# Order of the high products in feature-major steps, and four compression taps side by side

## The chip, the cores and the metric

The kernel runs on one core of a Trainium2 chip. The metric is the time of one execution on the device in microseconds. A core has TensorE (PE in the profile, its weight loads PEld), VectorE (DVE), ScalarE (ACT), GpSimd (POOL) and SyncE (SP, which here issues nearly all DMAs). Each runs its own instructions in order and waits for the others by semaphores.

## The reference

The reference is a decoder trunk of four layers on 256 tokens of 1024 features, float32. Each layer is `x = x + mixer(rms_norm(x))`, then `x = x + square(relu(rms_norm(x) @ w_up)) @ w_down` with 4096 hidden features. The mixers are native sparse attention (NSA), stick-breaking attention, a convolution module, and block-sparse attention.

What the change touches in the first mixer is the compression of keys and values. For 2 groups of heads, each of 15 windows of 32 tokens (a window starts every 16 tokens) is reduced to one vector:

```
n_cmp = (S - L) // STR + 1                      # 15, with L = 32 and STR = 16
cidx = cmp_start[:, None] + jnp.arange(L)[None, :]
kc = einsum('bnlgd,lde->bnge', kc[:, cidx] + cmp_pos[0][None, None, :, None, :], w_cmp[0])
vc = einsum('bnlgd,lde->bnge', vc[:, cidx] + cmp_pos[1][None, None, :, None, :], w_cmp[1])
...
p_c = _masked_softmax(einsum('bqghd,bngd->bqghn', qc, kc) * scale, ...)
o_c = einsum('bqghn,bngd->bqghd', p_c, vc)
```

So a window is a sum over 32 positions ("taps") of a token's vector plus a position vector, times that tap's own 128 x 128 matrix.

## The kernel before, in words

Activations are feature-major (features on partitions) in `xr`. Every projection is made of float32r products: weights arrive by DMA as float32 (`raw`, 1 MB, three buffers), ACT rounds them to a high part `wh` (L155) and DVE subtracts to a low part `wl` (L156); activations are split the same way, and three products are summed: high by high, high by low, low by high.

`proj_T` makes feature-major results. It is used for the up projections of all four MLPs and for queries and keys of the stick-breaking layer. `wh` is the stationary operand against both parts of the activations at once (512 columns, L200), `wl` against the high part (256 columns, L201). Two features of 128 rows are made together, each in its own PSUM bank: in each of the eight steps `kt` first the one feature's two products are issued, then the other's. `proj` makes token-major results with three products of 512 columns (`mm3`, L180 to L182), as the down projection does.

NSA runs as six column chunks of its projection: keys and values for the compression (chunk 0, transposed to `kcT` by `transpose_to`), the other keys (1), four heads of queries (2), values and gates (3), the remaining heads (4, 5). `compress` stands between chunk 3 and the first `attend`. For keys and then values, DVE adds the position vectors to all windows (`win`, L532, two instructions), and 32 float32 matmuls of 30 columns by 128 (L540) sum the taps in PSUM (`pc`); a float32 matmul is two records in the trace. The taps' matrices come in four transfers of 1 MB (`rawc`, L537) into the same three `raw` buffers. For the keys the result is copied (`kk`), transposed and copied into columns 256 to 286 of `kcat`, which `scores` reads; between products and copy, `flush` issues twelve pending transposes (L450). For the values it is copied to `vcmp`, which `mix` reads.

`attend` goes through units (head, half of the tokens): `scores` (mask and score products, maxima on DVE, exponentials on ACT, weights on DVE) and one unit later `mix` (transposes and value products). A scheduler at build time sets the final order on each engine; so products of chunks 4 and 5 stand between the units' instructions.

Of the kernel before, what the change touches and what calls it, by code (L numbers as in the profile page):

```python
# [10 lines left out]
F32 = mybir.dt.float32  # L11
# [55 lines left out]
def trunk(ctx: ExitStack, tc: tile.TileContext, A: dict, out: bass.AP):  # L67
# [8 lines left out]
    def bank(tag, name):  # L76
        return ps.tile([P, 512], F32, tag=tag, bufs=4 if tag == "B" else 2, name=name)
# [116 lines left out]
    def proj_T(aT, v, fs):  # L194

        os_ = [bank("B", "projT") for f in fs]
        for kt in range(KT):
            for o, f in zip(os_, fs):
                c = slice(f * P, (f + 1) * P)
                nc.tensor.matmul(o, lhsT=v[kt][0][:, c], rhs=aT[:, kt], start=kt == 0, stop=False)  # L200
                nc.tensor.matmul(o[:, :S], lhsT=v[kt][1][:, c], rhs=aT[:, kt, 0], start=False, stop=kt == KT - 1)  # L201
        return os_
# [211 lines left out]
    def nsa(n, first):  # L414
        aT = n.xT
        nxt = start_norm(4)
        with tc.tile_pool(name="nsa", bufs=1) as sp:
# [13 lines left out]
            nc.vector.memset(kcat[:, :, 256:288], 0.0)  # L431
            nc.vector.memset(vcmp, 0.0)
            oT = act.tile([P, KT, 2, NT, P], F32R, tag="aT", name="oT")
            with tc.tile_pool(name="nsw", bufs=2) as wp:
# [11 lines left out]
                def transpose_to(dsts, srcs):  # L446
                    def go():
                        pt = bank("B", "pt")
                        for i, s_ in enumerate(srcs):
                            nc.tensor.transpose(pt[:, i * P:(i + 1) * P], s_, ident)  # L450
                        for d_, (a, b) in dsts:
                            nc.scalar.copy(d_, pt[:, a * P:b * P].rearrange("p (a b) -> p a b", b=P))

                    waiting.append(go)
# [9 lines left out]
                kcT = wp.tile([P, 2, 2, S], F32, tag="kcT", bufs=1, name="kcT")  # L464
# [5 lines left out]
                def chunk(ci):  # L470
# [10 lines left out]
                    for t in range(NT):  # L481
# [4 lines left out]
                        if ci == 0:  # L486
# [5 lines left out]
                            transpose_to([(kcT[:, 0, :, ts_], (0, 2)), (kcT[:, 1, :, ts_], (2, 4))],  # L492
# [24 lines left out]
                def tables():  # L517
                    nc.sync.dma_start(mks, A["nsa_mask"])
                    nc.vector.tensor_copy(mk, mks)
                    nc.gpsimd.tensor_copy(identr, ident)  # L520
                    nc.sync.dma_start(posT, A["nsa_pos"])

                def compress():

                    for kv in range(2):
                        win = wp.tile([P, 960], F32, tag="win", bufs=1, name="win").rearrange(
                            "p (l g n) -> p l g n", g=2, n=15)
                        kc = kcT[:, kv]
                        for g in range(2):
                            src = bass.AP(tensor=kc.tensor, offset=kc.offset + g * S,  # L530
                                          ap=[kc.ap[0], [1, 32], [16, 15]])
                            nc.vector.tensor_tensor(win[:, :, g], src,  # L532
                                                    posT[:, kv, :, None].to_broadcast([P, 32, 15]), op=ALU.add)
                        pc = bank("B", "pc")
                        for hf in range(2):
                            raw = rawp.tile([P, 2048], F32, tag="raw", name="rawc")
                            nc.sync.dma_start(raw, A["nsa_cmp"][:, kv, hf * 2048:(hf + 1) * 2048])  # L537
                            for l in range(16):
                                ll = hf * 16 + l
                                nc.tensor.matmul(pc[:30, :DH], lhsT=win[:, ll].rearrange("p a b -> p (a b)"),  # L540
                                                 rhs=raw[:, l * DH:(l + 1) * DH], start=ll == 0, stop=ll == 31)
                        if kv == 0:
                            flush()
                            kk = wp.tile([32, DH], F32, tag="kk", bufs=1, name="kk")
                            nc.scalar.copy(kk[:30], pc[:30, :DH])
                            pt = bank("B", "pt")
                            nc.tensor.transpose(pt[:, :30], kk[:30], ident[:30, :30])
                            for g in range(2):
                                nc.scalar.copy(kcat[:, g, 256:286], pt[:, :30])
                        else:  # L550
                            nc.scalar.copy(vcmp[:30], pc[:30, :DH])
# [95 lines left out]
                compress()  # L647
                attend([(h, t) for t in range(NT) for h in range(4)])
# [421 lines left out]
def _constants():  # L1070
# [14 lines left out]
    for t in range(NT):  # L1085
        for g in range(2):
            m = np.full((P, 32), NEG)
            for n in range(15):
                m[:, 15 * g + n] = np.where(16 * n + 31 <= t * P + i, 0.0, NEG)
            mask.append(m)  # L1090
# [3 lines left out]
    tri = np.stack([np.where(i[:, None] >= i[None, :], -1.0, 0.0), np.full((P, P), -1.0)], 1).astype(np.float32)  # L1094
    return {
        "ident": np.eye(P, dtype=np.float32), "rope": rope, "causal": causal,
# [4 lines left out]
def _layout(x):  # L1101
# [23 lines left out]
    a["nsa_cmp"] = np.ascontiguousarray(f["nsa_w_cmp"][0].transpose(2, 0, 1, 3).reshape(P, 2, -1))  # L1125
# [37 lines left out]
```

## Time and profile before

| | |
|---|---|
| median of 3 runs (lowest, highest) | 1221.04 us (1220.31, 1221.4) |
| the profiled execution: its own time, its span | 1220.13 us, 1218.2 us |
| PE busy | 1196.0 us (98%), 7009 records |
| weight loads busy | 1023.7 us (84%) |
| DVE busy | 781.0 us (64%) |
| ACT busy | 628.4 us (52%) |
| POOL busy | 28.3 us (2%) |
| read from HBM | 207.73 MB, 172 GB/s over the span |
| mean granted clock of TensorE | 0.997 |

Matmuls overlap: a record's duration is longer than the distance to the next start. What a matmul costs in a dense stream is read from start to start. The timeline merges neighbours of one line and shape; "x64" are then 64 records from the first start to the last end.

### The profile page before, as it was taken

To read this page: it belongs to the slowest core of one execution; us is meant where nothing else is said; L and a number is where in the kernel's file an instruction comes from. 1 tells how busy PE (TensorE), PEld (TensorE's weight loads), DVE (VectorE), ACT (ScalarE), POOL (GpSimd) and SP (SyncE) were. 2 spreads that over 40 slices of the span, in tenths; PEclk is the share of its full clock that TensorE was granted. 3 is DMA by queue.
4 is the path that set the end of the run, shared out by engine and by line. 5 is a ranking of instruction groups with operands and counts; after the bars stand their busy time and mean duration, and the time that the engine had idled before them with its cause. 6 is when DMAs were issued, how large, how long until landed. Compare 5 with 4: busy or idle time off the path is not lost.

```text
span 1218.2 us, 17586 instructions
## 1 busy us (share of the span) xinstructions
PE 1196.0 (98%) x7009; PEld 1023.7 (84%) x7009; DVE 781.0 (64%) x1208; ACT 628.4 (52%) x1035; POOL 28.3 (2%) x36
## 2 busy tenths in 40 slices
PE   7999999999999999999999989999999999999998
PEld 5888888888888898888888869888888879888887
DVE  7877685565585479555665258655657886755563
ACT  6376664444465555444563256444446655545341
POOL 0100000000000000000000000000001010000000
PEclk9999999999999999999999989999999999999999
DMA  7544064554554425554546326545544643545540
GB/s 288 183 174 163 16 231 169 207 203 147 203 181 153 162 90 202 199 206 171 189 160 255 123 78 246 185 173 207 199 144 174 238 139 105 207 155 196 202 173 35
DMA packets 33777, 211.09 MB, mean 173 GB/s; under 512 B 4256, under 2 KB 6304, under 8 KB 10144
## 3 DMA queue, kind: packets, MB, share of 16 engines
q1 hardware_dynamic: 31104, 203.99, 46.9%
q0 software_dynamic: 1152, 4.70, 1.1%
q10 hardware_dynamic: 1440, 1.28, 0.3%
q8 instruction: 55, 0.90, 0.3%
q14 instruction: 26, 0.21, 0.0%
HBM read 207.73 MB, written 2.23 MB: 172 GB/s over the span
## 4 chain that ended last, share of the span: by engine, by line
PE 92%; DVE 4%; ACT 1%; POOL 1%; DMA 1%; issue 1%; SPq 0%; ACTq 0%; DVEq 0%; POOLq 0%
PE projT L200 22%; PE projT L201 11%; PE dn L180 10%; PE dn L182 10%; PE dn L181 10%; PE ab L859 4%; PE proj L180 3%; PE proj L181 3%; PE proj L182 3%; PE acc L207 3%; PE acc L208 2%; PE acc L209 2%; PE cv L793 2%; DVE wl L156 2%; PE pc L540 1%; PE po L626 1%
## 5 line engine op out<-in xcount | busy, mean ns | idle before, releaser
L156 DVE TENSOR_TENSOR wl<-raw,wh 128x1024 fp32r<-128x1024 f32 (+2 forms) x376 | 445.7, 1210 | 205.3 <-ACT wh L155 204.7
L155 ACT CAST wh<-raw 128x1024 fp32r<-128x1024 f32 (+2 forms) x376 | 379.7, 1041 | 213.3 <-PE dn L182 112.5
L200 PE MATMUL projT<-xT,wh 128*128 128x512 f32 x1152 | 407.9, 398 | 0.3 <-DVE xT L100 0.3
L201 PE MATMUL projT<-xT,wl 128*128 128x256 f32 x1152 | 323.0, 281 | 0.0
L200 PEld LDWEIGHTS projT<-xT,wh 128*128 128x128 f32 x1152 | 216.3, 188 | 53.0 <-DVE xT L100 0.5
L201 PEld LDWEIGHTS projT<-xT,wl 128*128 128x128 f32 x1152 | 217.4, 189 | 1.1
L180 PE MATMUL dn<-wh,u 128*128 128x512 f32 x512 | 201.4, 393 | 0.0
L182 PE MATMUL dn<-wh,u 128*128 128x512 f32 x512 | 200.3, 391 | 0.0
L181 PE MATMUL dn<-wl,u 128*128 128x512 f32 x512 | 200.1, 391 | 0.0
L182 PEld LDWEIGHTS dn<-wh,u 128*128 128x128 f32 x512 | 96.2, 188 | 21.2
L180 PEld LDWEIGHTS dn<-wh,u 128*128 128x128 f32 x512 | 96.2, 188 | 20.5
L181 PEld LDWEIGHTS dn<-wl,u 128*128 128x128 f32 x512 | 96.3, 188 | 19.6
L300 ACT COPY b<-projT 128x256 f32<-128x256 f32 x128 | 46.9, 373 | 93.2 <-PE projT L201 89.5
L180 PE MATMUL proj<-wh,xT 128*128 128x512 f32 (+2 forms) x224 | 87.0, 389 | 7.7 <-ACT wh L155 7.7
L181 PE MATMUL proj<-wl,xT 128*128 128x512 f32 (+2 forms) x224 | 86.0, 384 | 0.0
L182 PE MATMUL proj<-wh,xT 128*128 128x512 f32 (+2 forms) x224 | 85.3, 382 | 0.0
L301 DVE TENSOR_TENSOR s<-projT,b 128x256 f32<-128x256 f32 x128 | 51.4, 421 | 50.3 <-ACT b L300 50.1
L88 ACT CAST u<-q 128x1024 fp32r<-128x1024 f32 x32 | 33.6, 1050 | 82.1 <-DVE q L303 82.1
L207 PE MATMUL acc<-oT,wh 128*128 128x256 f32 x256 | 74.0, 294 | 1.9 <-ACT oT L88 1.9
L208 PE MATMUL acc<-oT,wh 128*128 128x256 f32 x256 | 74.1, 291 | 0.4 <-DVE oT L89 0.4
L209 PE MATMUL acc<-oT,wl 128*128 128x256 f32 x256 | 71.6, 288 | 0.0
L89 DVE TENSOR_TENSOR u<-q,u 128x1024 fp32r<-128x1024 f32 x32 | 39.2, 1225 | 33.5 <-ACT u L88 33.5
(257 smaller groups left out, 1273.7 us busy)
## 6 DMA issues: line engine op xcount, KB each, us to landing
raw<-in_up SPq DMA_DIRECT2D x64, 1024.0 KB, 4.8
raw<-in_down SPq DMA_DIRECT2D x64, 1024.0 KB, 4.9
raw<-in_sb_w SPq DMA_DIRECT2D x12, 1024.0 KB, 4.8
raw<-in_moba_w SPq DMA_DIRECT2D x12, 1024.0 KB, 4.9
raw<-in_conv_w SPq DMA_DIRECT2D x8, 1024.0 KB, 4.9
st<-dr POOLq DMA_DIRECT2D x8, 574.0 KB, 4.2
raw<-in_nsa_w SPq DMA_DIRECT2D x4, 1024.0 KB, 5.9
rawc<-in_nsa_cmp SPq DMA_DIRECT2D x4, 1024.0 KB, 5.0
```

What stands on the lines that cost most here:

```text
L155: nc.scalar.copy(wh[:, :w], r)
L156: nc.vector.tensor_sub(wl[:, :w], r, wh[:, :w].bitcast(F32))
L180: nc.tensor.matmul(o, lhsT=aT[:, kt, 0, t, :], rhs=wh, start=first, stop=False)
L181: nc.tensor.matmul(o, lhsT=aT[:, kt, 0, t, :], rhs=wl, start=False, stop=False)
L182: nc.tensor.matmul(o, lhsT=aT[:, kt, 1, t, :], rhs=wh, start=False, stop=last)
L200: nc.tensor.matmul(o, lhsT=v[kt][0][:, c], rhs=aT[:, kt], start=kt == 0, stop=False)
L201: nc.tensor.matmul(o[:, :S], lhsT=v[kt][1][:, c], rhs=aT[:, kt, 0], start=False, stop=kt == KT - 1)
L207: nc.tensor.matmul(o, lhsT=wh, rhs=aT[:, kt, 0], start=first, stop=False, skip_group_check=True)
L208: nc.tensor.matmul(o, lhsT=wh, rhs=aT[:, kt, 1], start=False, stop=False, skip_group_check=True)
L209: nc.tensor.matmul(o, lhsT=wl, rhs=aT[:, kt, 0], start=False, stop=last, skip_group_check=True)
L301: nc.vector.tensor_add(s[:, f], o[:, :S], b)
L859: nc.tensor.matmul(os_[f][:, i * S:(i + 1) * S], lhsT=v[kt][wi][:, fs], rhs=aT[:, kt, xi], start=kt == 0 and m == 0 and i == 0, stop=kt == ...
```

## The change

In `proj_T` the loop over the two features moves inside the loop over the two parts: high, high, low, low instead of high, low, high, low.

In NSA `kcT` changes its layout: for each of 16 residues r of the token number there are 36 columns; columns 1 to 32 hold the 16 tokens `16 n + r` of both groups, column 0 and column 33 the two position vectors of taps r and 16 + r, the rest is zero. A slice of 32 neighbouring columns is then a stationary operand as it stands, and no windows are built. Four taps go to four groups of 32 output rows of one PSUM bank; their sum, with the shift by one window and the position vectors' products, is made by one more matmul with a constant 0/1 matrix `quarters`, which for the keys also transposes. Position vectors and zeros are written by POOL, `quarters` comes by its own DMA of 16 KB. The masks and the order of the tap matrices in memory are permuted to match. `compress(1)`, the values' part, is called before the second unit of `attend`.

```
 def proj_T(aT, v, fs):
         for kt in range(KT):
-            for o, f in zip(os_, fs):
-                c = slice(f * P, (f + 1) * P)
-                nc.tensor.matmul(o, lhsT=v[kt][0][:, c], rhs=aT[:, kt], start=kt == 0, stop=False)
-                nc.tensor.matmul(o[:, :S], lhsT=v[kt][1][:, c], rhs=aT[:, kt, 0], start=False, stop=kt == KT - 1)
+            for part, width in enumerate((2 * S, S)):
+                rhs = aT[:, kt] if part == 0 else aT[:, kt, 0]
+                for o, f in zip(os_, fs):
+                    nc.tensor.matmul(o[:, :width], lhsT=v[kt][part][:, f * P:(f + 1) * P], rhs=rhs,
+                                     start=kt == 0 and part == 0, stop=kt == KT - 1 and part == 1)
...
-                kcT = wp.tile([P, 2, 2, S], F32, tag="kcT", bufs=1, name="kcT")
+                kcT = wp.tile([P, 2, 16, 36], F32, tag="kcT", bufs=1, name="kcT")
...
-                            transpose_to([(kcT[:, 0, :, ts_], (0, 2)), (kcT[:, 1, :, ts_], (2, 4))],
+                            cols = [kcT[:, kv, :, 1 + 16 * t:17 + 16 * t].rearrange("p r (n g) -> p g n r", g=2)
+                                    for kv in range(2)]
+                            transpose_to([(cols[0], (0, 2)), (cols[1], (2, 4))],
...
                     nc.sync.dma_start(posT, A["nsa_pos"])
+                    nc.sync.dma_start(quarters, A["cmp_sum"])
+                    nc.gpsimd.memset(kcT[:, :, :, 34:36], 0.0)
+                    nc.gpsimd.tensor_copy(kcT[:, :, :, 0:34:33], posT.rearrange("p k (a r) -> p k r a", a=2))
...
-                def compress():
-                    for kv in range(2):
-                        win = wp.tile([P, 960], F32, tag="win", bufs=1, name="win").rearrange(
-                            "p (l g n) -> p l g n", g=2, n=15)
...
-                            nc.vector.tensor_tensor(win[:, :, g], src,
-                                                    posT[:, kv, :, None].to_broadcast([P, 32, 15]), op=ALU.add)
...
-                                nc.tensor.matmul(pc[:30, :DH], lhsT=win[:, ll].rearrange("p a b -> p (a b)"),
-                                                 rhs=raw[:, l * DH:(l + 1) * DH], start=ll == 0, stop=ll == 31)
...
+                def compress(kv):
+                    pc = bank("B", "pc")
+                    for hf in range(2):
+                        raw = rawp.tile([P, 2048], F32, tag="raw", name="rawc")
+                        nc.sync.dma_start(raw, A["nsa_cmp"][:, kv, hf * 2048:(hf + 1) * 2048])
+                        for k in range(16):
+                            r, a = divmod(k, 2)
+                            j = 64 * a + 32 * (r % 2)
+                            nc.tensor.matmul(pc[j:j + 32, :DH], lhsT=kcT[:, kv, 8 * hf + r, 3 * a:3 * a + 32],
+                                             rhs=raw[:, k * DH:(k + 1) * DH], start=hf == 0 and r < 2,
+                                             stop=hf == 1 and r >= 6, skip_group_check=True)
+                    if kv == 0:
+                        flush()
+                    part = wp.tile([P, DH], F32, tag="part", name="part")
+                    nc.scalar.copy(part, pc[:, :DH])
+                    pt = bank("B", "pt")
+                    if kv == 0:
+                        nc.tensor.matmul(pt[:, :32], lhsT=part, rhs=quarters, start=True, stop=True)
                         for g in range(2):
+                            nc.scalar.copy(kcat[:, g, 256:288], pt[:, :32])
+                    else:
+                        nc.tensor.matmul(pt[:32, :DH], lhsT=quarters, rhs=part, start=True, stop=True)
+                        nc.scalar.copy(vcmp, pt[:32, :DH])
...
-                compress()
-                attend([(h, t) for t in range(NT) for h in range(4)])
+                compress(0)
+                attend([(h, t) for t in range(NT) for h in range(4)], {1: lambda: compress(1)})
...
+    quarters = np.zeros((4, 32, 32), np.float32)
+    n = np.arange(30)
+    quarters[:2, n + 1, n] = quarters[:2, 0, :30] = 1.0
+    quarters[2:, n, n] = quarters[2:, 30, :30] = 1.0
```

On PE, one step in `proj_T` of the first MLP's up projection and the beginning of the next, before (`projT_1822` and `projT_1823` are the two features' banks, `wh` and `wl` with one number pair one piece of weights):

```order
L200 MATMUL projT_1822<-xT_86,wh_1807 128x512
L201 MATMUL projT_1822<-xT_86,wl_1808 128x256
L200 MATMUL projT_1823<-xT_86,wh_1807 128x512
L201 MATMUL projT_1823<-xT_86,wl_1808 128x256
L200 MATMUL projT_1822<-xT_86,wh_1807 128x512
```

The same place now (both products stand in line 201):

```order
L201 MATMUL projT_1822<-xT_86,wh_1807 128x512
L201 MATMUL projT_1823<-xT_86,wh_1807 128x512
L201 MATMUL projT_1822<-xT_86,wl_1808 128x256
L201 MATMUL projT_1823<-xT_86,wl_1808 128x256
L201 MATMUL projT_1822<-xT_86,wh_1807 128x512
```

The two wide products now stand together and the two narrow ones behind them, and the bank changes with every product.

On PE, from the end of chunk 3 to the second unit's scores, before (`m_388`, `m_479`, `m_491` are the last keys and the two halves of the queries, `sc` a unit's scores):

```order
L182 MATMUL proj<-wh,xT 128x280
L540 MATMUL pc<-rawc,win 30x128 x32
L450 MATMUL pt<-ident,m_388 128x128 x4
L450 MATMUL pt<-ident,m_479 128x128 x4
L450 MATMUL pt<-ident,m_491 128x128 x4
L547 MATMUL pt<-ident,kk 128x30
L540 MATMUL pc<-rawc,win 30x128 x32
L563 MATMUL sc<-mk,identr 128x32
L565 MATMUL sc<-mk,identr 128x256
L567 MATMUL sc<-kcat,qT 128x288
L563 MATMUL sc<-mk,identr 128x32
```

And now:

```order
L182 MATMUL proj<-wh,xT 128x280
L544 MATMUL pc<-rawc,kcT 32x128 x32
L450 MATMUL pt<-ident,m_390 128x128 x4
L450 MATMUL pt<-ident,m_481 128x128 x4
L450 MATMUL pt<-ident,m_493 128x128 x4
L553 MATMUL pt<-quarters,part 128x32
L570 MATMUL sc<-mk,identr 128x32
L572 MATMUL sc<-mk,identr 128x256
L544 MATMUL pc<-rawc,kcT 32x128 x8
L574 MATMUL sc<-kcat,qT 128x288
L544 MATMUL pc<-rawc,kcT 32x128 x24
L557 MATMUL pt<-part,quarters 32x128
```

The values' products have gone in between and behind the first unit's scores, and the sum of the values' quarters (L557) stands in front of all further scores.

On ACT, from the copy of the keys' result to the first exponentials, before:

```order
L545 COPY kk<-pc 30x128
L452 COPY kcat<-pt 128x2x128 x2
L452 COPY qT<-pt 128x4x128 x2
L549 COPY kcat<-pt 128x30 x2
L155 CAST wh<-raw 128x768 x2
L551 COPY vcmp<-pc 30x128
L155 CAST wh<-raw 128x768 x2
L599 ACTIVATE pr,sums<-sc,nm,rq 128x128 x2
L599 ACTIVATE pr,sums<-sc,nm,rq 128x32
```

And now:

```order
L550 COPY part<-pc 128x128
L455 COPY kcat<-pt 128x2x128 x2
L455 COPY qT<-pt 128x4x128 x2
L555 COPY kcat<-pt 128x32 x2
L606 ACTIVATE pr,sums<-sc,nm,rq 128x128 x2
L606 ACTIVATE pr,sums<-sc,nm,rq 128x32
L550 COPY part<-pc 128x128
L558 COPY vcmp<-pt 32x128
L155 CAST wh<-raw 128x768
L626 COPY PT<-pp 128x256
```

The values' copy stands behind the first unit's exponentials, and the four weight casts of chunk 4, which stood ahead of them, stand behind.

## Rows read from the trace of the kernel before

**Rows 1.** The page, busy time by engine and chain by line.

```profile
PE 1196.0 (98%) x7009; PEld 1023.7 (84%) x7009; DVE 781.0 (64%) x1208; ACT 628.4 (52%) x1035; POOL 28.3 (2%) x36
...
PE projT L200 22%; PE projT L201 11%; PE dn L180 10%; PE dn L182 10%; PE dn L181 10%; PE ab L859 4%; PE proj L180 3%; PE proj L181 3%; PE proj L182 3%; PE acc L207 3%; PE acc L208 2%; PE acc L209 2%; PE cv L793 2%; DVE wl L156 2%; PE pc L540 1%; PE po L626 1%
```

**Rows 2.** The page's groups: the wide products of `proj_T` (count, mean ns).

```profile
L200 PE MATMUL projT<-xT,wh 128*128 128x512 f32 x1152 | 407.9, 398 | 0.3 <-DVE xT L100 0.3
```

**Rows 3.** Timeline of PE, start of an up projection: start us, us, what.

```profile
301.09 0.39 PE L200 MATMUL projT<-xT,wh 128*128 128x512 f32 x1
301.31 0.28 PE L201 MATMUL projT<-xT,wl 128*128 128x256 f32 x1
301.43 0.40 PE L200 MATMUL projT<-xT,wh 128*128 128x512 f32 x1
...
305.67 0.40 PE L200 MATMUL projT<-xT,wh 128*128 128x512 f32 x1
```

**Rows 4.** Timeline of PE, a token-major projection (`proj`) of NSA.

```profile
32.57 0.39 PE L180 MATMUL proj<-wh,xT 128*128 128x512 f32 x1
...
41.18 0.39 PE L182 MATMUL proj<-wh,xT 128*128 128x512 f32 x1
```

**Rows 5.** Timeline of PE, convolution layer: products of 256 columns, then column groups.

```profile
654.90 0.28 PE L859 MATMUL ab<-xT,wl 128*128 128x256 f32 x1
...
661.38 0.28 PE L859 MATMUL ab<-xT,wl 128*128 128x256 f32 x1
661.59 7.11 PE L793 MATMUL cv<-st,taps 128*32 128x256 f32 x128
668.63 0.51 PE L859 MATMUL ab<-xT,wh 128*128 128x256 f32 x2
```

**Rows 6.** Timeline of PE, end of an up projection: first down products.

```profile
312.38 0.40 PE L180 MATMUL dn<-wh,u 128*128 128x512 f32 x1
312.62 0.40 PE L181 MATMUL dn<-wl,u 128*128 128x512 f32 x1
```

**Rows 7.** Timeline of PE, the compression.

```profile
51.39 7.17 PE L540 MATMUL pc<-rawc,win 128*30 128x128 f32 x64
58.49 1.53 PE L450 MATMUL pt<-ident,m 128*128 128x128 f32 x12
59.95 0.24 PE L547 MATMUL pt<-ident,kk 30*128 30x30 f32 x1
60.77 7.15 PE L540 MATMUL pc<-rawc,win 128*30 128x128 f32 x64 [0.57 <-DVE win L532]
67.84 0.28 PE L563 MATMUL sc<-mk,identr 128*128 128x32 f32 x1
```

**Rows 8.** Timeline of DVE ahead of the compression's end.

```profile
46.30 1.00 DVE L532 TENSOR_TENSOR win<-kcT,posT 128x480 f32<-128x480 f32 x1
...
55.27 0.69 DVE L392 TENSOR_TENSOR m<-m,m 128x512 f32<-128x512 f32 x1
```

**Rows 9.** Timeline of ACT, compression and first unit.

```profile
60.67 0.32 ACT L549 COPY kcat<-pt 128x30 f32<-128x30 f32 x2
62.78 1.56 ACT L155 CAST wh<-raw 128x768 fp32r<-128x768 f32 x2 [1.79 <-DMA raw<-in_nsa_w]
...
70.72 0.46 ACT L599 ACTIVATE pr<-sc,nm,rq 128x128 f32<-128x128 f32 x1 [0.51 <-DVE nm L595]
...
71.86 0.20 ACT L599 ACTIVATION_READ_ACCUMULATOR pr<-sc,nm,rq 128x1 f32 x1
```

**Rows 10.** Timeline of SP's queue, the fourth transfer of tap matrices.

```profile
55.10 0.33 SPq L537 DMA_DIRECT2D rawc<-in_nsa_cmp  x1
```

**Rows 11.** The page, DMA issues (count, KB, us to landing).

```profile
rawc<-in_nsa_cmp SPq DMA_DIRECT2D x4, 1024.0 KB, 5.0
```

**Rows 12.** Groups by form, whole span: the first reduction of a unit.

```profile
L569 DVE TENSOR_REDUCE mx<-sc 128x2 f32<-128x256 f32 x8 | 3.3, 414 | 3.4 <-PE sc L567 3.4
```

**Rows 13.** Busy time of each engine in the attention's first 12 us.

```profile
68.00:80.00 12.00, 12.00 (x75) 10.38 (x76) 10.42 (x46) 10.98 (x43) 0.00 (x0) 1.00 0.58 216
```

More of the change, by code (lines that the diff above doesn't have):

```diff
@@ L430, in nsa @@
             vcmp = sp.tile([32, DH], F32, name="vcmp")
-            nc.vector.memset(kcat[:, :, 256:288], 0.0)
-            nc.vector.memset(vcmp, 0.0)
+            quarters = sp.tile([P, 32], F32, name="quarters")
             oT = act.tile([P, KT, 2, NT, P], F32R, tag="aT", name="oT")
@@ L451, in go @@
                         for d_, (a, b) in dsts:
-                            nc.scalar.copy(d_, pt[:, a * P:b * P].rearrange("p (a b) -> p a b", b=P))
+                            v = pt[:, a * P:b * P].rearrange("p (a b) -> p a b", b=P)
+                            if len(d_.shape) == 4:
+                                v = v.rearrange("p a (n r) -> p a n r", r=16)
+                            nc.scalar.copy(d_, v)
                     waiting.append(go)
@@ L521, in tables @@
                     nc.sync.dma_start(posT, A["nsa_pos"])
-                def compress():
-                    for kv in range(2):
-                        win = wp.tile([P, 960], F32, tag="win", bufs=1, name="win").rearrange(
-                            "p (l g n) -> p l g n", g=2, n=15)
-                        kc = kcT[:, kv]
-                        for g in range(2):
-                            src = bass.AP(tensor=kc.tensor, offset=kc.offset + g * S,
-                                          ap=[kc.ap[0], [1, 32], [16, 15]])
-                            nc.vector.tensor_tensor(win[:, :, g], src,
-                                                    posT[:, kv, :, None].to_broadcast([P, 32, 15]), op=ALU.add)
[L534 to L539, printed above, removed]
-                                nc.tensor.matmul(pc[:30, :DH], lhsT=win[:, ll].rearrange("p a b -> p (a b)"),
-                                                 rhs=raw[:, l * DH:(l + 1) * DH], start=ll == 0, stop=ll == 31)
[L542 to L551, printed above, removed]
@@ L1088, in _constants @@
             for n in range(15):
-                m[:, 15 * g + n] = np.where(16 * n + 31 <= t * P + i, 0.0, NEG)
+                m[:, 2 * n + g] = np.where(16 * n + 31 <= t * P + i, 0.0, NEG)
             mask.append(m)
@@ L1094, in _constants @@
     tri = np.stack([np.where(i[:, None] >= i[None, :], -1.0, 0.0), np.full((P, P), -1.0)], 1).astype(np.float32)
+    quarters = np.zeros((4, 32, 32), np.float32)
+    n = np.arange(30)
+    quarters[:2, n + 1, n] = quarters[:2, 0, :30] = 1.0
+    quarters[2:, n, n] = quarters[2:, 30, :30] = 1.0
     return {
+        "cmp_sum": quarters.reshape(P, 32),
         "ident": np.eye(P, dtype=np.float32), "rope": rope, "causal": causal,
@@ L1124, in _layout @@
     a["nsa_pos"] = np.ascontiguousarray(f["nsa_cmp_pos"][0].transpose(2, 0, 1))
-    a["nsa_cmp"] = np.ascontiguousarray(f["nsa_w_cmp"][0].transpose(2, 0, 1, 3).reshape(P, 2, -1))
+    a["nsa_cmp"] = np.ascontiguousarray(
+        f["nsa_w_cmp"][0].reshape(2, 2, 16, DH, DH).transpose(3, 0, 2, 1, 4).reshape(P, 2, -1))
     thirds = [[(b + 512 * h, b + 512 * h + 512)] for h in range(2) for b in (0, 1024, 2048)]
```

## The prediction

> **What bounds the kernel now.** First the totals: PE (TensorE's matmul row) is busy 1196.0 of 1218.2 us, and a third of the chain that ended last is the two lines of `proj_T` [rows 1]. So what counts is how fast PE issues, read from start to start, since a matmul's own duration overlaps its neighbours. Then PE in time, in the four kinds of stretch that the change touches.
>
> Inside `proj_T` a long product (high weights, 512 columns) and a short one (low weights, 256) alternate, 1152 of each [rows 2]. Twelve pairs lie between 301.43 and 305.67 us: 353 ns a pair [rows 3]. Long ones alone follow each other every 227 ns (38 between 32.57 and 41.18) [rows 4], short ones alone every 120 ns (54 between 654.90 and 661.38) [rows 5], together 347. So alternating loses 6 ns a pair. Where: the first long product of a run, behind a long one of the down projection, takes 0.22 us although a short one follows (301.09 to 301.31) [rows 3]; behind the run's last short one a long product takes 0.24 although long ones follow (312.38 to 312.62) [rows 6]. The dear place is the long product behind a short one.
>
> The compression is two runs of 32 matmuls, two records each: 7.10 us from 51.39 to 58.49 and 7.07 us from 60.77 to 67.84, 111 ns a record; there the scores begin [rows 7]. The convolution shows what column groups do: 128 records of 32 columns by 256 take 7.04 us from 661.59 to 668.63 [rows 5], 55 ns each or 220 ns for a round of four, that is the stream of one record alone.
>
> **Order of the high and low products.** Nothing is added or removed. Of four products one long one instead of two stands behind a short one. By the steady rates 227 + 227 + 120 + 120 = 694 and one loss of 6 gives 700 ns against 706: 576 fours x 6 ns = **3.5 us saved**, all on the path, since PE is the chain. Ends: 0, if the loss belongs to each short product; 6.9 us, if it vanishes. No row shows two short products behind two long ones, nor the other side, a change of PSUM bank after every product (rival below). Each pair of results is complete one product later; the next pair has two other banks, so nobody waits.
>
> **The taps.** I compare the stretch from 51.39 to the first scores at 67.84, 16.45 us [rows 7], with what its work would take now; the score units themselves stay as they are, some of them between the products.
> - Products: 128 records in 32 rounds of four. A round can't be shorter than one record's 111 ns: 3.6 us. If a record needs 55 ns whatever its width, as in the convolution, 7.0. I take 3.6, since there the round took just the columns' stream.
> - Twelve transposes unchanged, 58.49 to 59.95, 1.5 us [rows 7]. Two small matmuls with `quarters` for one transpose of `kk`, 0.2 us each as an estimate from the 0.24 of that record [rows 7]: 0.4. Entering and leaving column groups costs about 0.1 us each time (661.38 to 661.59 is 0.21 where 0.12 is usual [rows 5]); three more changes: 0.3. Together 5.8 us.
> - Waits, from the order of instructions. (a) The last four transposes need the second query rope, which ended at 55.96 [rows 8]; two `win` additions of 1.0 us each stood before it on DVE (a second one like the row shown), so about 54.2 now, and PE is there at 54.2: 0.2. (b) `kcat` is copied 1.04 us after the transposes' end (59.95 to 60.99) [rows 7, 9]; formerly the values' products covered it, now masks and eight products, about 1.0 us: 0.1. (c) The fourth tap transfer was issued at 55.10, as the first half's products ended, and a transfer takes 5.0 us [rows 10, 11]. The buffer now frees at 52.3, so it lands near 57.5, and PE comes at about 56.9: 0.6. (d) The values' sum waits on ACT behind the first unit's exponentials: DVE 0.8 (0.41 for the first reduction [rows 12], 0.2 each for two smaller ones, an estimate), then 1.35 us on ACT (70.72 to 72.06 [rows 9]), then the copy `part`, 0.25. That makes 59.05 where PE is done at 58.4: 0.65. Behind it on PE all further scores queue. Sum of waits 1.6 us.
> - So 7.4 us instead of 16.45: 9.0 saved.
> - Given back: the attention then starts earlier against ACT, which is busy 10.98 of 12 us there [rows 13]. Two weight casts that ran before it (62.78, 1.56 us [rows 9]) now fall inside, and one more copy of 0.25. If PE waits for all of it 1.8 us, if its projections cover it none, and with a chain of several units 3. I take 1.0.
>
> **Saved: 8.0 us** (bounds in the rivals). The later two `win` additions cost PE 0.57 us before 60.77 [rows 7], which is inside the 16.45.
>
> **At nothing**: the strided copies into `kcT` on ACT (they come with chunk 1, two chunks ahead of their first reader at 51.39 [rows 7]); on POOL the filling and the copy of `posT` ahead of the reciprocal roots, hidden behind the arrival of the first products' statistics, and if the 32 KB came late every later step would move with it; the extra 16 KB transfer on SP's queue, issued while the queue waits for weight buffers anyway. If their covers failed, each would cost under 0.5 us.
>
> A rule that speaks against the taps: [rows 5] hold four records in 220 ns on the same 128 rows, though each has its own weight load. The Trainium skill ("TensorE: Matmul & The Clock Gate", Part 3, The mechanism) says that a weight load overlaps running matmuls only when its row group differs, and here all four share the rows. By that rule the products would keep their 14.2 us; the rows above disagree with it at 256 columns, and 128 columns no run here shows.
>
> **Sum.** The profiled execution took 1220.13 us (span 1218.2 and 1.9 around it). 1220.1 - 3.5 - 8.0 = 1208.6. The median shown, 1221.04, lies 0.9 us above that execution; by it the result is 1209.5. I predict 1209.
>
> **Rivals** (times from 1220.1).
> 1. *The order does nothing*: the 6 ns belong to each short product. For it: a short product in the pairs takes 0.12 us (301.31 to 301.43 [rows 3]), no less than among its like. Against: the long products behind short ones in [rows 6]. 1220.1 - 8.0 = 1212.
> 2. *The taps' gain is half lost*: rounds of 220 ns (7.0 for 3.6 us) and ACT costing 3 instead of 1. For it: ACT's 10.98 of 12 us. Against: PE has two projections to fill in. 1220.1 - 3.5 - 2.6 = 1214.
> 3. *More than forecast*: no loss at all in the fours, no wait for ACT: 1220.1 - 6.9 - 9.0 = 1204.
> 4. *Slower*: the new order changes the PSUM bank after every product instead of every second one, 1152 more changes. If one costs more than 8.0 us / 1152 = 7 ns, the kernel is no faster; at 10 ns it is 1220.1 - 8.0 + 11.5 = 1223.6. For it: the 6 ns lost per pair would then be today's price of one change. Against: `proj` changes bank at every third product and still runs at 227 ns [rows 4].
> 5. *Each tap pays for its own weight load*: products stay at 14.2 and cover waits (a) and (c), so 16.45 becomes 14.2 + 2.2 + 0.75 = 17.15, and nothing starts earlier: 1220.1 - 3.5 + 0.7 = 1217.3, which is no change that can be measured. The page named above would lead there.
>
> **How the numbers follow.** Forecast 50%, rival 1 17%, rival 2 15%, rival 3 8%, rival 4 7% (5 slower, 2 within), rival 5 3%. About 0.2% or 2.4 us is what a measurement of this kernel can tell from no change. Faster: 50 + 17 + 15 + 8 = 90%; within: 5%; slower: 5%. The forecast's own range is 1206 to 1211.5; with rivals 1, 2 and 3 it becomes 1203.5 to 1216, which leaves rivals 4 and 5 and the edges out.
>
> **What would show it.** Right: in `proj_T` a four takes about 700 ns, with only the first long product above 230; the taps start in rounds of four some 111 ns apart, two runs of about 1.8 us; PE idles before the fourth transfer and before the values' sum; the first scores start near 56 us instead of 67.8. Wrong: a four still at 706 or more; rounds at 220 ns; an attention stage that ends less than 6 us earlier than now; or a gain elsewhere, since nothing else is touched.

## The result, and the profile after

The changed kernel takes 1207.74 us (median of 4 runs, 1207.02 to 1209.31) against 1220.67 of the kernel before: a ratio of 0.9895, 95% interval 0.9878 to 0.9912. Run again later, its median was 1206.23, ratio 0.9885 (0.9869 to 0.9900). The forecast was 1209. The profiled execution took 1208.27 us; the page of it, busy time and chain, to be held against [rows 1]:

```profile
span 1206.2 us, 17585 instructions
PE 1182.4 (98%) x7012; PEld 1012.6 (84%) x7012; DVE 779.4 (65%) x1202; ACT 626.6 (52%) x1036; POOL 29.9 (2%) x38
...
PE 89%; DVE 5%; DMA 2%; ACT 2%; POOL 1%; issue 1%; SPq 0%; ACTq 0%; DVEq 0%; POOLq 0%
...
PE projT L201 33%; PE dn L180 10%; PE dn L182 10%; PE dn L181 10%; PE ab L866 3%; PE acc L208 3%; PE acc L209 2%; PE acc L210 2%; PE proj L180 2%; PE proj L182 2%; PE proj L181 2%; PE cv L800 2%; DVE wl L156 2%; PE po L633 1%; DMA st<-dr 1%
```

PE is still what ends last, with 13.6 us less of it. New at the end of the chain is a transfer, `st<-dr`: it belongs to the convolution, which the change does not touch.

A whole run of `proj_T`, 64 products, from the first to the down product behind it (timeline of PE):

```profile
204.60 0.61 PE L201 MATMUL projT<-xT,wh 128*128 128x512 f32 x2
205.05 0.40 PE L201 MATMUL projT<-xT,wl 128*128 128x256 f32 x2
205.28 0.63 PE L201 MATMUL projT<-xT,wh 128*128 128x512 f32 x2
...
215.51 0.39 PE L201 MATMUL projT<-xT,wl 128*128 128x256 f32 x2
215.73 0.40 PE L180 MATMUL dn<-wh,u 128*128 128x512 f32 x1
```

204.60 to 215.73 is 11.13 us where before had 11.29 (301.09 to 312.38, [rows 3, 6]): 696 ns a four, not 706. The compression and the first unit, timeline of PE, which answers to [rows 7]:

```profile
52.45 1.95 PE L544 MATMUL pc<-rawc,kcT 128*32 128x128 f32 x64
54.34 1.64 PE L450 MATMUL pt<-ident,m 128*128 128x128 f32 x12
55.81 0.31 PE L553 MATMUL pt<-quarters,part 128*128 128x32 f32 x2
55.95 0.26 PE L570 MATMUL sc<-mk,identr 128*128 128x32 f32 x1
56.07 0.36 PE L572 MATMUL sc<-mk,identr 128*128 128x256 f32 x1
56.36 0.65 PE L544 MATMUL pc<-rawc,kcT 128*32 128x128 f32 x16
56.93 0.75 PE L574 MATMUL sc<-kcat,qT 128*128 128x288 f32 x2
57.62 1.88 PE L544 MATMUL pc<-rawc,kcT 128*32 128x128 f32 x48
60.18 0.41 PE L557 MATMUL pt<-part,quarters 128*32 128x128 f32 x2 [0.69 <-ACT part L550]
60.52 0.28 PE L570 MATMUL sc<-mk,identr 128*128 128x32 f32 x1
```

The keys' 64 records take 1.89 us to the next start instead of 7.10, and the first masks stand at 55.95 instead of 67.84. The wait at 60.18 is the one forecast as (d); on ACT the copy stands behind the first unit's last exponential:

```profile
59.51 0.37 ACT L606 ACTIVATE pr<-sc,nm,rq 128x32 f32<-128x32 f32 x1
59.78 0.20 ACT L606 ACTIVATION_READ_ACCUMULATOR pr<-sc,nm,rq 128x1 f32 x1
59.87 0.26 ACT L550 COPY part<-pc 128x128 f32<-128x128 f32 x1
```

Now the transfer. The chain of waits of the changed kernel in the convolution:

```profile
643.30 3.61 DMA dr<-upad
646.90 0.30 issue
647.20 9.05 DMA st<-dr
656.26 0.14 issue
656.39 0.62 PE cv L800 x6
```

Each channel of the convolution is written to memory (`dr<-upad`, issued by ACT) and read back in stacked form (`st<-dr`, 574 KB, issued by POOL). POOL's timeline, before and then now:

```profile
656.04 1.26 POOL L782 DMA_DIRECT2D st<-dr  x2 [6.17 <-ACT wh L155]
```

```profile
645.34 0.72 POOL L789 DMA_DIRECT2D st<-dr  x1 [6.23 <-ACT wh L155]
647.20 0.55 POOL L789 DMA_DIRECT2D st<-dr  x1 [1.14 <-DMA dr<-upad]
```

Before issued the reads of the first two channels together. Now the second one waits for its write, goes out just ahead of two weight transfers of 1 MB (issued from 647.38) and takes 9.05 us; PE waits 1.90 us for it.

By stretch of PE, in us, each from the starts of its products in the profiled executions (the convolution from the first transposes of the MLP's results ahead of it; the last line is the rest of the span):

| stretch | before | changed | order alone | taps alone |
|---|---|---|---|---|
| start to the first tap | 51.39 | 52.45 | 51.48 | 52.94 |
| first tap to the first up projection | 103.10 | 94.95 | 103.01 | 95.18 |
| convolution, up to its output projection | 93.03 | 95.15 | 95.40 | 95.16 |
| everything else | 970.68 | 963.64 | 963.58 | 970.86 |

So 8.15 us came from the taps and 7.0 from the order, 15.2 in all; 1.06 went ahead of the first tap and 2.12 in the convolution, which leaves 12.0. The last line is good to some 0.8 us: second profiles of the same two kernels (below) have 969.92 and 964.22 there. Summed from start to start, the products of `proj_T` and the down products are about 6.5 us shorter in either pair.

### The profile page after: what moved, and what is told of

It is laid out like the page before. It is cut to its first block, busy times and chain, and to the rows that moved or that the text cites. A ratio compares the mean times of both kernels' runs of the same rounds, so it can differ in the third digit from the quotient of the medians.

```text
span 1206.2 us, 17585 instructions
## 1 busy us (share of the span) xinstructions
PE 1182.4 (98%) x7012; PEld 1012.6 (84%) x7012; DVE 779.4 (65%) x1202; ACT 626.6 (52%) x1036; POOL 29.9 (2%) x38
## 4 chain that ended last, share of the span: by engine, by line
PE 89%; DVE 5%; DMA 2%; ACT 2%; POOL 1%; issue 1%; SPq 0%; ACTq 0%; DVEq 0%; POOLq 0%
PE projT L201 33%; PE dn L180 10%; PE dn L182 10%; PE dn L181 10%; PE ab L866 3%; PE acc L208 3%; PE acc L209 2%; PE acc L210 2%; PE proj L180 2%; PE proj L182 2%; PE proj L181 2%; PE cv L800 2%; DVE wl L156 2%; PE po L633 1%; DMA st<-dr 1%
## 5 line engine op out<-in xcount | busy, mean ns | idle before, releaser
L201 PE MATMUL projT<-xT,wh 128*128 128x512 f32 x1152 | 361.3, 396 | 0.3 <-DVE xT L100 0.3
L201 PE MATMUL projT<-xT,wl 128*128 128x256 f32 x1152 | 225.6, 278 | 0.0
L201 PEld LDWEIGHTS projT<-xT,wh 128*128 128x128 f32 x1152 | 178.3, 189 | 3.5 <-DVE xT L100 0.5
L301 ACT COPY b<-projT 128x256 f32<-128x256 f32 x128 | 41.3, 374 | 92.5 <-PE projT L201 92.5
L302 DVE TENSOR_TENSOR s<-projT,b 128x256 f32<-128x256 f32 x128 | 48.1, 418 | 54.0 <-ACT b L301 54.0
```

The lines of the kernel that those rows point to most:

```text
L201: nc.tensor.matmul(o[:, :width], lhsT=v[kt][part][:, f * P:(f + 1) * P], rhs=rhs, start=kt == 0 and part == 0, stop=kt == KT - 1 and part ...
L301: nc.scalar.copy(b, o[:, S:])
L302: nc.vector.tensor_add(s[:, f], o[:, :S], b)
```

## The experiments

Ten other kernels ran, and each of the two once more. Each median stands against one of before, measured along with it: 1220.65 for order alone, taps alone, two banks, and four and four; 1220.67 for the changed kernel again, one column group, values first, and the copy on DVE; 1219.96 for before again, the two with the joint write, and crossed.

**One part at a time.** Order alone is before with the new loop in `proj_T`; taps alone is the changed kernel with the old one.

> The kernel before with nothing changed but the order in proj_T (high, high, low, low). Theory A (the traces of before and after: the 16 fours of a run fell from 11.29 to 11.14 us, and the down products behind a run no longer pay anything back): the order alone is worth 6 to 7 us, about 1214.0. Theory B (the prediction's step: one loss of 6 ns in a four instead of two, 576 times): 3.5 us, 1217.2, and the rest of the gain comes with the taps. Rival (the order does nothing): 1220.7.

> The changed kernel with the old order in proj_T (high, low for the one feature, then for the other). Theory A: the taps are worth 6 to 7 us, about 1214.0, and the two parts add up. Theory B: 9.5 us, 1211.2. If the convolution's late transfer (2 us in the profiled run of the changed kernel) comes from the shifted start, it stays here; if it is chance, it comes and goes between runs.

Order alone: 1214.75, ratio 0.9948 (0.9934 to 0.9961). Taps alone: 1215.00, 0.9952 (0.9940 to 0.9965). In the table above each moves its own stretch and not the other's: 7.10 us for the order, 7.92 for the taps. Both lose over 2 us in the convolution, order alone too, where nothing ahead of the first MLP differs. So the parts add up as theory A had it, theory B's split did not come, and the medians stand above what the parts are worth by themselves; for the taps even A was too low.

**Three other orders in `proj_T`**, all in the changed kernel. Two banks:

```
-for part, width in ...:  for o, f in zip(os_, fs): ...
+for o, f in list(zip(os_, fs))[::-1 if kt % 2 else 1]:   # h0 l0 h1 l1 | l1 h1 h0 l0 | l0 h0 h1 l1 ...
+    for part in ((0, 1) if kt == 0 else (last, 1 - last)): ...
```

> The changed kernel with the four products of a step in an order that walks back and forth between the two features, so that narrow products still stand in pairs and wide ones in pairs, but the bank changes once in four products instead of four times. Theory A (what costs is the change between wide and narrow): no change against the changed kernel, 1207.7 within 0.7. Rival (a change of bank costs about 1 ns, a quarter of the 3.7 ns that a four still loses): 576 x 3 x 0.9 ns = 1.6 us less, 1206.1. Other rival (two records in a row on one bank cost, which would be what the old order paid for): 3 us more, 1211.

Four and four:

```
-for kt in range(KT):  for part ...: for o, f ...
+for k2 in range(0, KT, 2):
+    for part, width in enumerate((2 * S, S)):
+        for kt in (k2, k2 + 1):  for o, f in zip(os_, fs): ...
```

> The changed kernel with two steps of proj_T taken together: four wide products, then four narrow ones. Theory A (the loss belongs to the change between wide and narrow, 3.7 ns in a four of 697.7): half as many changes, 576 x 1.85 ns = 1.1 us less, 1206.6. Rival (the rest of the loss belongs to each product or to the bank): no change, 1207.7. Slower by a microsecond or more if weights of the second step arrive too late.

Crossed (the first step still high, high, low, low):

```
+if kt: seq = [s for k in range(len(fs)) for s in ((0, k), (1, k ^ 1))]     # h0 l1 h1 l0
```

> The changed kernel with the four products of a step as wide of the one feature, narrow of the other, wide of the other, narrow of the one. Theory (the loss comes with each change between wide and narrow, whatever the bank): 64 products take 11.29 us as in the old order, and the kernel is 6 us slower than the changed one, 1213. Rival (the loss of the old order comes from two records in a row on one bank, or from banks that change only every second product): 11.14 us, 1207.

The first product of the run of 64 that answers to the one shown, and the down product behind it, first two banks, then four and four, then crossed:

```profile
204.73 0.39 PE L204 MATMUL projT<-xT,wh 128*128 128x512 f32 x1
...
215.90 0.39 PE L180 MATMUL dn<-wh,u 128*128 128x512 f32 x1
```

```profile
203.75 1.07 PE L202 MATMUL projT<-xT,wh 128*128 128x512 f32 x4
...
214.95 0.40 PE L180 MATMUL dn<-wh,u 128*128 128x512 f32 x1
```

```profile
204.34 0.62 PE L204 MATMUL projT<-xT,wh 128*128 128x512 f32 x2
...
215.62 0.40 PE L180 MATMUL dn<-wh,u 128*128 128x512 f32 x1
```

| order in a step | 64 products | starts, steady, ns (wide, narrow) | median, ratio (interval) |
|---|---|---|---|
| before: w n w n, bank 0 0 1 1 | 11.29 | 232 to 241, 113 to 120 | |
| changed: w w n n, bank 0 1 0 1 | 11.13 | 231 to 236, 112 to 119 | 1207.74, 0.9895 (0.9878 to 0.9912) |
| two banks: w n n w, one bank change | 11.17 | 224 to 237, 112 to 121 | 1209.05, 0.9902 (0.9888 to 0.9915) |
| four and four | 11.20 | 224 to 236, 116 to 120 | 1211.45, 0.9923 (0.9911 to 0.9935) |
| crossed: w n w n, bank 0 1 1 0 | 11.28 | 232 to 241, 113 to 120 | 1211.64, 0.9930 (0.9917 to 0.9942) |

Starts are distances from one start to the next. Crossed has in this run the old order's time and even its pattern of starts (233, 241, 236 for the wide ones, over and over) with other banks: the loss goes with wide and narrow in turn, and the bank does not matter to it. Two banks against changed: fewer bank changes give nothing. But four and four should then have been the best, and it is worse than two and two: its narrow products run at 116 to 120, up to the rate of narrow ones among themselves, and its wide ones mostly at 233 to 236. So there is no fixed price for a change between wide and narrow, as theory A had it: it would be 3 ns in the old order (four changes lose 12 in 706), 1 in two and two (two changes lose 2 in 696), 6 in four and four (two changes lose 12 in eight products of 1400). What makes pairs best stays open.

Nor does wide and narrow in turn always lose. The kernel before, in a run of 64 products of the stick-breaking layer (timeline of PE):

```profile
395.68 0.40 PE L200 MATMUL projT<-xT,wh 128*128 128x512 f32 x1
...
406.08 0.40 PE L200 MATMUL projT<-xT,wh 128*128 128x512 f32 x1
```

Thirty pairs in 10.40 us: 347 ns a pair, the sum of the steady rates, with wide ones at 230 to 233. Of the 32 runs of 58 products or more in that profile three go like this, the others at 353 or over; one of the three, at 381 us, takes 353 in before's second profile. In crossed three runs of the second MLP take 11.12 us, at 347 too. So an order does not fix the price: the same products in the same order settle at one of two rates, mostly the slower one, and what decides it is not shown. Two and two stays within 1 ns of 697 a four in all such runs of the changed kernel but one (702).

**The changed kernel again.**

> The changed kernel as it is, once more, with a second profile. If its two parts add up (order alone 5.9 us, taps alone 5.65 us) it stands near 1209.0; if they help each other, at 1207.7 as first measured. Theory (the convolution's late transfer of 2 us is chance): its profile shows the wait there in some executions and not in others, and the start of the taps moves by the 0.44 us that each microsecond of a later clock rise costs. Rival (the wait belongs to the change): the same 1.9 us at the same place.

1206.23, below both values named; its profile has the wait in the convolution (1.6 us) and the wait for DVE described below (0.4), and the first tap at 51.33, because the products' spacing fell from 0.43 to 0.23 us (the granted clock rose from the lower to the higher level) at 11.0 us and not at 13.8. First tap to first up projection: 95.00.

**One column group.**

```
-j = 64 * a + 32 * (r % 2)
+j = 0
```

> The changed kernel with all 32 taps summed in the same 32 output rows instead of in four groups side by side (the sum of quarters takes 32 rows; so the windows' shift and half of the position sums are left out). Theory (the gain of the taps is that four stream at once): a record costs 111 ns again, two runs of 7.1 us instead of 1.9, minus the waits that they now cover (0.5 to 1.2 us): about 9.5 us more than the changed kernel, 1217.5. Rival (the gain came from the windows that DVE no longer builds, or from the moved order): about 1208.

1219.69 (eleven runs, 1216.73 to 1222.16), ratio 0.9991 (0.9982 to 1.0001): the gain of the whole change is gone, and more was lost than expected. The timeline of PE:

```profile
52.66 7.17 PE L544 MATMUL pc<-rawc,kcT 128*32 128x128 f32 x64
59.76 1.53 PE L450 MATMUL pt<-ident,m 128*128 128x128 f32 x12
```

109 ns a record, as before the change. First tap to first up projection takes 104.66 us, 9.7 more than in the changed kernel, as the theory had it; the rest of the difference lies in the convolution (95.98) and ahead of the taps. Same slices, same DVE work, same place in the program: what the change gains here is the four streams side by side.

**The values' part in its old place.**

```
 compress(0)
+compress(1)
-attend([...], {1: lambda: compress(1)})
+attend([...])
```

> The changed kernel with the values' part of the compression called right behind the keys' part, ahead of all scores. Theory (PE is what ends last, and the moved products are the same work in another place): within 0.7 us of the changed kernel. Rival (the first units' chain over DVE and ACT is what the move is for): first scores start some 2.5 us later and the attention ends 1.5 to 2.5 us later, about 1210. Other rival (the wait for ACT at the values' sum, 0.7 us, goes and nothing comes for it): 0.7 us faster.

1208.46, ratio 0.9903 (0.9890 to 0.9917), not to be told from the changed kernel by its time. By the stretch it is 1.5 us slower, 96.43 against 94.95, which is the first rival's size: the first masks start 7.90 us behind the first tap instead of 3.50. But something that nobody had named stands at the same place. PE, and the windows (busy us of PE, PEld, DVE, ACT, POOL, then the granted clock):

```profile
55.52 1.08 PE L544 MATMUL pc<-rawc,kcT 128*32 128x128 f32 x32
58.04 1.08 PE L544 MATMUL pc<-rawc,kcT 128*32 128x128 f32 x32 [1.45 <-DMA rawc<-in_nsa_cmp]
```

```profile
59.95:63.30 3.35, 3.35 (x11) 2.78 (x12) 1.06 (x4) 2.52 (x7) 0.00 (x0) 0.50 0.89 350
```

With no scores to put in between, PE waits 1.45 us for the fourth transfer of tap matrices and 0.38 at the values' sum, and behind that idle time the granted clock is 0.50, the lower level, for 3.4 us. In the changed kernel masks and scores fill most of that time. How much of the 1.5 us is the clock and how much the later scores, this run does not separate.

**The copy on DVE.**

```
-nc.scalar.copy(part, pc[:, :DH])
+(nc.scalar.copy if kv == 0 else nc.vector.tensor_copy)(part, pc[:, :DH])
```

> The changed kernel with the copy of the values' quarters (part) on DVE instead of ACT, where it stands behind the first unit's exponentials. Theory (PE waits 0.7 us at the values' sum for ACT): the wait shrinks to 0.2 us or less and the kernel gains 0.4 us or nothing that can be measured. Rival (the scores behind it wait for ACT or DVE anyway): the idle time turns up at a later product, no change.

1209.87, 0.9914 (0.9900 to 0.9927). The wait did not shrink:

```profile
59.81 0.41 PE L557 MATMUL pt<-part,quarters 128*32 128x128 f32 x2 [0.80 <-DVE part L550]
```

DVE issues the copy at 59.47, behind an instruction that waits 1.50 us for the same exponentials. The stretch is 94.51, 0.4 shorter all the same; but in the profiled execution the convolution took 98.61, with a wait of 3.8 us and 3.4 us at a granted clock of 0.50 behind it, and that outweighs the edit.

**The convolution's wait.** First the kernel before once more; then the changed kernel with one write for two channels:

```
-(("stack", 0),), (("stack", 1),),        # write 0, read 0; write 1, read 1
+(), (("pair", 0),),
+nc.scalar.dma_start(<both channels>, up[:, ch:ch + 2])     # one write, then two reads
```

> The kernel before, one look with a second profile. Theory (the convolution's wait for its second stacked load is chance, and the first profile of before happened to lack it, as eight of the nine profiles taken since have 1.6 to 3.8 us of it): the wait is there, and the span stands at 1219 to 1220. Rival (the wait came with an earlier or later start, so with the change): no wait, span 1218.2 as before.

> The changed kernel with the convolution's first two channels written to memory by one transfer, so that the first stacked load can't start between the two writes. Theory (the first load, 574 KB, starts at 2.4 us after the first write and makes the second write land late, so that the second load is issued beside two weight transfers of 1 MB): the wait of 1.6 to 3.8 us goes, 1.5 to 2 us faster than the changed kernel, near 1205.5. Rival (the second load is late because of the weight transfers, however early the write lands): no change, 1206 to 1208.

Before again took 1219.33 us (one run) and has no wait: the theory of pure chance is not borne out, though two profiles without it do not rule it out. Of the ten profiles of other kernels that write the two channels apart, eight have a wait of 1.6 to 3.8 us; two (four and four, crossed) have none. What differs shows in the packets. The DMA queues (packets, MB, share of 16 engines): of before, from 1.85 us behind the issue of the first write on; of the changed kernel, from 1.30 to 1.85 us behind it, and from there on:

```profile
q8 instruction: 1, 0.02, 4.4%
q10 hardware_dynamic: 3, 0.00, 0.1%
```

```profile
DMA packets 147, 0.16 MB, mean 290 GB/s; under 512 B 22, under 2 KB 146, under 8 KB 146
...
q8 instruction: 1, 0.02, 14.4%
```

```profile
DMA packets 10, 0.01 MB, mean 6 GB/s; under 512 B 2, under 2 KB 10, under 8 KB 10
...
q10 hardware_dynamic: 10, 0.01, 3.2%
```

One packet of 16,384 bytes on the instruction queue, taking 1.0 to 1.9 us. In before it starts 1.87 us after the first write was issued, again 2.24, when the last of the writes' 288 packets have gone (1.88, again 1.94). In the eight profiles with the wait it starts at 0.99 to 1.70. In seven of these 279 packets are done by 1.9 and the last nine trail until 3.2 to 4.1; nine is a sixteenth of one write's 144, one of 16 engines' share. The first of the nine starts where the instruction packet ends: 3.37 and 3.38 us for order alone, 2.73 and 2.74 for the changed kernel, and in all seven, and in four and four, within 0.02 us. So they stood behind it. The first read is not what holds them up, as the theory had it: in the changed kernel its first packet starts at 3.84, when the nine are through (3.48). The second read then goes out at 4.0 to 4.9 instead of 3.1, and the weight transfers at 4.46. (In four and four it starts at 1.38, but the read is out at 3.90 and PE does not wait; with taps alone it is out at 3.97 and PE waits 1.93, so how late is too late is a matter of less than 0.1 us or of something else. In crossed the packet comes ahead of the writes. In the copy on DVE the packet came earliest of the eight, and both reads went out late.) All this is read from the times of packets, not tested by moving the packet; why it comes 0.2 to 0.9 us earlier is open. Order alone has it too, with no instruction more or less on PE.

With the joint write the wait is gone from the profile (convolution 93.57; also from that of the next kernel, 93.71), and the profiled execution took 1207.04 us. The median is 1208.44, 0.9903 (0.9887 to 0.9919): of six runs three lie at 1205.9 to 1207.0 and three at 1209.8 to 1211.6. What the second three did is open; only the first was profiled. So the 1.5 to 2 us that the theory promised are not shown by the time.

**Joint write and a later sum**: the values' sum is called ahead of the first `mix`.

```
+late.append(total)          # total: the matmul with quarters and the copy to vcmp
 def mix(h, t, pr):
+    while late: late.pop()()
```

> The same with the joint write, and the sum of the values' quarters called only ahead of the first unit's mix, so that the second unit's scores no longer stand behind its wait for ACT (0.76 us). Theory (PE is what ends last and the second unit's scores fill the wait): from the first tap to the first up projection 94.3 us instead of 95.0, and 0.7 us faster than with the joint write alone. Rival (ACT's exponentials set the pace of the first units): the wait turns up behind, 95.0 as before.

```profile
57.43 0.65 PE L546 MATMUL pc<-rawc,kcT 128*32 128x128 f32 x16
58.01 0.28 PE L574 MATMUL sc<-mk,identr 128*128 128x32 f32 x1
...
58.92 1.08 PE L546 MATMUL pc<-rawc,kcT 128*32 128x128 f32 x32
60.66 0.41 PE L560 MATMUL pt<-part,quarters 128*32 128x128 f32 x2 [0.66 <-ACT part L552]
```

1205.44 (1205.15 to 1206.46), 0.9879 (0.9865 to 0.9894), the lowest median of all, though its interval overlaps that of the changed kernel. The stretch is 94.37 as expected. The wait for ACT is as long as it was, but the second unit's scores now stand ahead of it, and cover the wait for the fourth transfer.

## Why the prediction was right, and where it was not

The time came out within 1.3 us by luck: errors on both sides nearly cancelled, and not each term held.

| term | predicted | measured |
|---|---|---|
| order in `proj_T` | -3.5 | -7.0 |
| first tap to first up projection | -8.0 | -8.15 |
| ahead of the first tap | 0 | +1.06 |
| convolution | 0 | +2.12 |

**The order.** That it counts and that it lies on the path was right; the size was not. The step that failed is "the dear place is the long product behind a short one", with one loss of 6 ns kept in every four. A four takes 696 ns, 2 over the steady rates and not 6, and both its wide products start above 230, not the first alone. Narrow ones run below their own 120 ns (112 to 119), and wide ones above their 227. The second omission: before's down products still pay behind a run (behind the one at 301 us the first four take 240, 238, 233 and 236 ns, from the records), where the changed kernel's are soon back at 227 (233, 231, 226). Inside the runs the order is worth 5.8 us (407.6 to 401.8 in all), and the down products take about 0.8 less (229.6 to 229.1 ns from start to start, over 1524 of them). So rival 3's term for the order, 6.9 with the loss gone, came nearest, though 2 ns in a four are left. A pair of rates taken in dense streams was no measure of a mix: the old order itself runs at either of two rates. Rival 1 fell with order alone, rival 4 with the two-bank order: a bank change has no price that shows.

**The taps.** Nearly every piece held. Within a round the records start 7, 7 and 7 ns apart and the next round 89 later: 110 ns for four, against the 111 forecast. Transposes 1.47 us (1.5). Entering or leaving column groups: 203 ns where a record otherwise has 110, 0.09 each (0.1). Waits: 0.1 for the query rope (0.2 forecast; the ninth transpose starts 190 ns behind the eighth, the usual distance is 109), none for `kcat` (0.1), 0.3 for the fourth transfer (0.6; one of the 48 records takes 421 ns to the next), 0.76 at the values' sum (0.65; 966 ns where 203 would do). So 0.4 us less waiting than forecast, and by the difference about 1.3 given back later instead of 1.0. Rival 2 fell with the rounds. Rival 5 fell with them too: the Trainium skill ("TensorE: Matmul & The Clock Gate", Part 3, The mechanism) lets a weight load overlap only where the row group differs. Here four records on the same rows, each with its own load, start within 21 ns; and one column group costs the full 109 ns each.

**At nothing, wrongly.** The copy of `posT` on POOL did hide: in all eleven profiles that have it the reciprocal roots behind it start 0.08 to 0.10 us after the DVE result that they wait for, as in before. (The copy's own record is 0.30 to 3.05 us long in these profiles, 2.66 in the first; that length says little.) But with other instructions around it the scheduler also set chunks 0 to 3 in another order, which neither the diff nor my reading of the order brought out, and PE waits in chunk 3 for DVE to free a bank:

```profile
46.03 0.40 PE L180 MATMUL proj<-wh,xT 128*128 128x280 f32 x1 [0.40 <-DVE qn L401]
```

All eleven profiles with the new compression have this wait (0.4 to 1.2 us); both of before and the one of order alone have none. Most of the other 0.66 us goes with the clock, whose granted level rose 1.35 us later; that goes up and down with nothing changed ahead of it (11.0 and 13.8 us in two profiles of the changed kernel). Among the nine new-compression profiles with a wait of about 0.4 us the first tap starts at 51.33 where the clock rose at 11.0 and at 52.66 where it rose at 14.1, about 0.4 us for each.

**"Nothing else is touched"** was wrong by 2.1 us. In program order it held, but not in time: the convolution had a race between a write and an instruction packet, and in both profiles of before the write won it by 0.3 us at most. That the change made it lose is not shown, since why the packet comes earlier is open.

## What to carry to other kernels

Where products of unequal width alternate, try pairs of like width, and measure the mix itself, in every run of it: rates from uniform streams gave half the gain, longer groups were worse, and one and the same order ran at two rates. Small products that fill only a few output rows are worth laying side by side in column groups when one constant product can sum them. Judge an edit of under 2 us by the stretch it touches, since a transfer hundreds of microseconds later can move the time by more.

## What the runs showed of the hardware

- Four float32 records of 32 columns by 128 in four column groups take 110 ns together, one alone in its group 109: here three of four were free. With 256 columns it was 220 ns [rows 5].
- An instruction packet of 16 KB took 1.0 to 1.9 us. Where it began while the writes ran, nine of their 288 packets started only as it ended, up to 2.2 us late (eight profiles; in the copy on DVE more of them were late). The Trainium skill ("Runtime: NRT & Kernel Launch", Instruction fetch mechanics) says that instructions stream in blocks of 16 KiB by DMA, at a cost that is mostly hidden. The size agrees with the packet here. Hidden from the engine it may be; the write packets that stood behind it paid, and in eight of these nine profiles PE waited 1.6 to 3.8 us at the end of that.
- PE's idle times of 1.45 and 0.38 us around the values' second half of products (values first) were followed by 3.4 us at the lower clock level, and so was one of 3.8 us in the convolution (the copy on DVE); the waits of 1.9 us (the changed kernel) and 2.7 us (one column group) in the convolution were followed by none.
- Products of 512 and 256 columns in turn ran at 353 ns a pair in most runs and at 347 in a few, in the same order and the same kernel.
